# A two-layer hybrid trunk: the S5 input projection turned round and moved by DMA, two later slots in TensorE's order

## The chip, the cores and the metric

One core of one Trainium2 chip. The metric is the device time of one execution in microseconds (us). Engines: PE is TensorE, PEld its weight loads, DVE VectorE, ACT ScalarE, POOL GpSimd, SP SyncE, which here does nothing but issue DMAs.

## The reference

Two layers over one sequence of 512 tokens with 1024 features, all in float32. `h = modulate(rms_norm(x))` feeds every mixer through slices of one input matrix; the change touches the S5 mixer, the compressed keys of the sparse attention and a norm.

```python
x = x + 0.5 * g1 * swiglu(modulate(rms_norm(x, norm_ffn1), sh1, sc1), ffn1_w_in, ffn1_w_out)
h = modulate(rms_norm(x, norm_mix), sh2, sc2)
u_pool, u_q, u_kv, u_gate, u_s5 = split(h @ w_in)          # u_s5: 256 features
# S5: 16 groups of 16 features, 64 complex states each
bu = einsum('gph,bsgh->bsgp', b_bar, u_s5)                 # then a linear scan over the tokens
y  = einsum('ghp,bsgp->bsgh', c_mat, states).real + d_skip * u_s5
# compressed keys: blocks of 32 tokens every 16
k_cmp = rope(rms_norm(gelu((blk + pe) @ w1) @ w2, k_norm[0]))
x = x + g2 * (concat(norm(pool), norm(nsa), norm(y_s5)) @ w_out)
x = x + 0.5 * g3 * swiglu(modulate(rms_norm(x, norm_ffn2), sh3, sc3), ffn2_w_in, ffn2_w_out)
```

## The kernel before

Features of the residual and of `h` lie on the 128 partitions in 8 blocks, tokens along the free axis. A product of two float32 matrices is three matmuls (`mm3`): each operand is split into a rounded high part and a rest, and high x high, high x low and low x high are added up in PSUM. Weights come from DRAM through four slots (a loader issues the DMA on SP; a splitter makes the high part on ACT and the low part on DVE or POOL).

The order of the work is found when the program is built. `Sched` (class of `K`) holds a modelled clock for each engine; the stages are generators that yield the modelled time at which their last result is there, and the one with the earliest time issues next. So each engine gets one fixed list, executed in order. `act`, `tt`, `ptt`, `mm`, `tr` and `dma` issue an instruction (ACT, DVE, POOL, matmul, transpose on PE, DMA on SP) and return its modelled end. Adding a slack to a yielded time makes a stage resume later in the list: `calm` adds 450, `bcast_rstd` gets `NSLACK` (300) or `N2SLACK` (1300). Nothing waits for these times on the chip. A slack moves only the place in the lists.

In `mixer` the stages around the change come in this order. The projections of the values and keys (`proj_t`: tokens as the stationary operand, 256 columns moving) run, then the S5 projection. It is `proj_t` four times (lines 1973 to 1982), with the stationary operand `bass.DynSlice(s, 128, 4)`: every fourth token, starting at s. 96 matmuls of 128x256 go into four banks, four ACT evictions (`a5_evac`) put them into `a5` with tokens on the partitions, and `s5_chain` (line 1811) turns them into `U` by 8 transposes on PE in two banks and two ACT evictions. `U` holds features and token phase on the partitions: partition 32s + i, 8 blocks j, 128 chunks c of four tokens.

Then come the first product of the compressed keys (`compress(0)`, 16 matmuls of 128x64), the pool projection (48 matmuls of 128x512), the compressed values, another key projection, the queries and the attention. `s5_half` (one per half q of the S5 groups) multiplies `E` by `U` (two times four float32 matmuls of 128x128, which are two records each), rotates (DVE and POOL), scans (DVE, line 1770, 8 scans per half) and ends in the `Y` matmuls. `compress_post` (line 1586) takes the compressed keys through gelu, the second product with `w2` (one 64x64 matmul, after `calm`), the norm and the rotation, splits them into a high part `kh` (ACT) and a rest `kl` (DVE) and transposes both on PE. `norm_half` (line 832) sums squares, gets a row of statistics from PE, broadcasts it over the partitions with one matmul with ones (`bcast_rstd`), scales, and hands `h` to the first projections. Index 1 is the norm before the mixers.

```python
t = yield from proj_t(us5, b[:, 0:256], bass.DynSlice(s, 128, 4), 256, s == 3)
t = tr(b[:, j * 128:(j + 1) * 128], a5[:, jj].rearrange("p s c -> p (s c)"), ident)
```

Of the kernel before, what the change touches and what calls it, by code (L numbers as in the profile page):

```python
# [25 lines left out]
AF = mybir.ActivationFunctionType  # L26
# [292 lines left out]
NSLACK = 300.0  # L319
N2SLACK = 1300.0  # L320
LAT = {"pe": 150.0, "act": 100.0, "dve": 100.0, "pool": 120.0}
# [99 lines left out]
def kernel(ctx, tc, xT, c, ada, ws, sp, mp, bc, w1, c_cols, ada_pe, cst, out):  # L421
# [4 lines left out]
    K = Sched()  # L426
# [86 lines left out]
    def calm(t):  # L513

        return t + SLACK
# [23 lines left out]
    def wbank():  # L539
        n = yield from banks.get()  # L540
        return pbank(n)
# [265 lines left out]
    def bcast_rstd(rs, nb, dg, o, slack=0):  # L807

        for j in range(nb):
            t = ts(dg[:, j * 128:(j + 1) * 128], ident, rs[:, j:j + 1], None, OP.mult)  # L810
        yield t + slack
        return mm(o, ones, dg[:, :nb * 128])
# [12 lines left out]
    def norm_half(st, half):  # L825
# [20 lines left out]
        t = yield from bcast_rstd(ms, 2, sq, pb[:, :256], N2SLACK if "ops" in st and half != st["order"][0] else NSLACK)  # L846
# [658 lines left out]
    def mixer(l, st, nxt, s5):  # L1505
# [80 lines left out]
        def compress_post(kv, bn, b, t):  # L1586
            yield t
            (tn, ge), (t2n, kd) = yield from tmpn(F32, F32R)
            yield calm(act(ge[:, :64], b[:, :64], AF.Gelu_apprx_tanh))
# [140 lines left out]
        a5 = area[:, 4:6, :].rearrange("p a c -> p (a c)").rearrange("p (j s c) -> p j s c", j=8, s=4)  # L1730
# [3 lines left out]
        a5_ev, s5y_ev, e_done = [Ev() for _ in range(4)], Ev(), Ev()  # L1734
# [76 lines left out]
        def s5_chain():  # L1811
            for e in a5_ev:
                yield e
            yield s5["ev"]
            for q in range(2):
                yield calm(K.now)
                bn, b = yield from wbank()
                for j in range(4):
                    jj = 4 * q + j
                    t = tr(b[:, j * 128:(j + 1) * 128], a5[:, jj].rearrange("p s c -> p (s c)"), ident)  # L1820
                yield t
                t = act(U[:, 4 * q:4 * q + 4, :], b.rearrange("p (j c) -> p j c", j=4))
                banks.put(bn, t)
            yield calm(t)
# [148 lines left out]
        us5 = [take("s5"), take("s5")]  # L1973
        def a5_evac(bn, b, t, s):
            yield t
            t = act(a5[:, :, s, :], b[:, 0:256].rearrange("p (j c) -> p j c", j=8))
            banks.put(bn, t)
            K.set(a5_ev[s], t)
        for s in range(4):
            bn, b = yield from bank()  # L1980
            t = yield from proj_t(us5, b[:, 0:256], bass.DynSlice(s, 128, 4), 256, s == 3)
            K.spawn(a5_evac(bn, b, t, s))
# [640 lines left out]
```

## Time and profile before

| | |
|---|---|
| median of 3 runs | 2045.11 us (2043.85 to 2047.16) |
| the profiled execution | 2049.2 us, span 2047.2 us |
| mean granted TensorE clock | 0.983 |
| PE busy | 1963.0 us (96%), 12698 matmuls |
| PEld busy | 1769.3 us (86%) |
| DVE / ACT / POOL busy | 1600.8 (78%) / 895.9 (44%) / 636.9 (31%) us |
| chain that ended last | PE 76%, DVE 15%, POOL 5%, issue 2%, ACT 2%, DMA 1% |

Times in the views count from the start of the span. A group of a timeline is a run of like instructions: its start, its length, and in square brackets how long the engine stood idle just before it and what released it. `s` and `p` are tiles in SBUF and in PSUM. Line numbers are those of the kernel before: L502 is `mm`, L518 `tr`, L453 `act`, L462 `tt`, L489 `ptt`, L596 `dma`, L1770 the scan. In the changed kernel all helpers lie two lines lower, the scan three.

### The profile page before, as it was taken

To read this page: it belongs to the slowest core of one execution; us is meant where nothing else is said; L and a number is where in the kernel's file an instruction comes from. 1 tells how busy PE (TensorE), PEld (TensorE's weight loads), DVE (VectorE), ACT (ScalarE), POOL (GpSimd) and SP (SyncE) were. 2 spreads that over 40 slices of the span, in tenths; PEclk is the share of its full clock that TensorE was granted. 3 is DMA by queue.
4 is the path that set the end of the run, shared out by engine and by line. 5 is a ranking of instruction groups with operands and counts; after the bars stand their busy time and mean duration, and the time that the engine had idled before them with its cause. 6 is when DMAs were issued, how large, how long until landed. Compare 5 with 4: busy or idle time off the path is not lost.

```text
span 2047.2 us, 32760 instructions
## 1 busy us (share of the span) xinstructions
PE 1963.0 (96%) x12698; PEld 1769.3 (86%) x12698; DVE 1600.8 (78%) x2690; ACT 895.9 (44%) x1622; POOL 636.9 (31%) x849
## 2 busy tenths in 40 slices
PE   5999999999999899999999989999999998999999
PEld 3788888898988898999989888999978888898989
DVE  7679777776778788888889796778578779686866
ACT  3422222242566453534455343535327565453533
POOL 5039201954644520000022390056457362000000
PEclk9999999999998899999989999999999998999999
DMA  7658767531101125445322222313211011413232
GB/s 303 219 202 295 261 227 256 186 113 54 62 32 52 53 75 184 163 166 192 125 97 93 93 100 97 134 53 134 80 37 53 21 52 55 142 63 124 87 110 73
DMA packets 71147, 251.66 MB, mean 123 GB/s; under 512 B 8016, under 2 KB 10448, under 8 KB 70480
## 3 DMA queue, kind: packets, MB, share of 16 engines
q1 hardware_dynamic: 70992, 249.58, 34.8%
q8 instruction: 99, 1.62, 0.3%
q14 instruction: 56, 0.46, 0.1%
HBM read 247.45 MB, written 2.10 MB: 122 GB/s over the span
## 4 chain that ended last, share of the span: by engine, by line
PE 76%; DVE 15%; POOL 5%; issue 2%; ACT 2%; DMA 1%; SPq 0%; DVEq 0%; ACTq 0%; POOLq 0%
PE p L502 74%; DVE s L462 8%; DVE s L466 5%; POOL s L489 5%; PE p L518 3%; ACT s L453 2%; DVE s L1770 1%; DVE s L471 0%; DMA s<-in_ws_dram 0%; DMA s<-in_x_dram 0%; DVE p L2063 0%; DVE s L2063 0%; DVE s L481 0%; DVE s L473 0%; SPq L596 0%
## 5 line engine op out<-in xcount | busy, mean ns | idle before, releaser
L502 PE MATMUL p<-s,s 128*128 128x256 f32 (+5 forms) x12022 | 1911.4, 320 | 71.3 <-DVE s L462 28.2
L502 PEld LDWEIGHTS p<-s,s 128*128 128x128 f32 (+2 forms) x12022 | 1696.5, 194 | 253.6 <-DVE s L462 34.6
L453 ACT ACTIVATE s<-s 128x1024 fp32r<-128x1024 f32 (+4 forms) x900 | 615.1, 711 | 786.9 <-PE p L502 450.2
L462 DVE TENSOR_TENSOR s<-s,s 128x1024 fp32r<-128x1024 f32 (+7 forms) x804 | 754.1, 963 | 251.1 <-ACT s L453 240.8
L489 POOL TENSOR_TENSOR s<-s,s 128x256 f32<-128x256 f32 (+12 forms) x399 | 358.7, 920 | 291.7 <-DVE s L473 119.8
L489 POOL TENSOR_TENSOR s<-s 128x256 f32<-128x256 f32 (+4 forms) x244 | 178.7, 738 | 498.0 <-ACT s L453 330.0
L453 ACT ACTIVATE s<-p 128x512 f32<-128x512 f32 (+9 forms) x361 | 180.2, 520 | 269.3 <-PE p L502 196.5
L462 DVE TENSOR_TENSOR s<-p,s 128x512 f32<-128x512 f32 (+8 forms) x325 | 192.1, 604 | 62.1 <-ACT s L453 40.2
L466 DVE SCALAR_TENSOR_TENSOR s<-s,s 128x1024 f32<-128x1024 f32 (+3 forms) x179 | 204.0, 1146 | 1.7 <-DMA s<-in_ada_dram 0.5
L466 DVE SCALAR_TENSOR_TENSOR s<-p,s,s 128x512 f32<-128x512 f32 (+2 forms) x210 | 128.3, 619 | 52.7 <-PE p L502 48.5
L462 DVE TENSOR_TENSOR s<-s 128x256 f32<-128x256 f32 (+4 forms) x157 | 80.3, 522 | 16.5 <-POOL s L489 6.2
L498 POOL TENSOR_SCALAR s<-s 128x128 f32<-128x128 f32 (+9 forms) x58 | 34.3, 610 | 184.6 <-PE p L502 161.7
L518 PE MATMUL p<-s,s 128*128 128x128 f32 (+1 forms) x548 | 80.2, 275 | 9.7 <-DVE s L462 7.4
L518 PEld LDWEIGHTS p<-s,s 128*128 128x128 f32 (+1 forms) x548 | 64.6, 140 | 20.6 <-DVE s L462 8.0
L453 ACT ACTIVATE s<-p,s 128x512 f32<-128x512 f32 (+3 forms) x132 | 69.3, 533 | 25.3 <-DVE s L2063 15.8
L498 POOL TENSOR_SCALAR s<-s,s 128x512 f32<-128x512 f32 (+3 forms) x128 | 65.8, 535 | 22.4 <-DVE s L462 15.2
L466 DVE SCALAR_TENSOR_TENSOR s<-s,s,s 128x256 fp32r<-128x256 f32 (+3 forms) x124 | 66.9, 557 | 0.3 <-ACT s L453 0.2
L2063 DVE CUSTOM_DVE_ANT_0 p<-p,s 128x512 f32<-128x512 f32 (+3 forms) x128 | 60.5, 503 | 3.3 <-PE p L502 2.3
L453 ACT ACTIVATE s<-s,s 128x256 fp32r<-128x256 f32 x80 | 39.0, 504 | 27.3 <-DVE s L466 27.1
L466 DVE SCALAR_TENSOR_TENSOR s<-s,s,p 128x256 f32<-128x256 f32 (+1 forms) x88 | 42.3, 498 | 4.4 <-PE p L502 3.7
L462 DVE TENSOR_TENSOR s<-s,p 128x512 f32<-128x512 f32 (+1 forms) x35 | 20.5, 589 | 18.1 <-PE p L502 18.1
L466 DVE SCALAR_TENSOR_TENSOR s<-s 128x256 f32<-128x256 f32 (+3 forms) x72 | 32.4, 468 | 2.0 <-ACT s L453 1.6
(36 smaller groups left out, 212.0 us busy)
## 6 DMA issues: line engine op xcount, KB each, us to landing
s<-in_ws_dram SPq DMA_DIRECT2D x304, 512.0 KB, 4.2
s<-in_ada_dram SPq DMA_DIRECT2D x143, 512.0 KB, 4.9
s<-in_w_dram SPq DMA_DIRECT2D x4, 1024.0 KB, 6.2
s<-in_x_dram SPq DMA_DIRECT2D x8, 256.0 KB, 5.2
out_dram<-s SPq DMA_DIRECT2D x16, 128.0 KB, 1.7
s<-in_ws_dram SPq DMA_DIRECT2D x4, 420.0 KB, 3.0
s<-in_c_dram SPq DMA_DIRECT2D x2, 512.0 KB, 5.0
s<-in_bc_dram SPq DMA_DIRECT2D x2, 512.0 KB, 5.7
```

What stands on the lines that cost most here:

```text
L453: nc.scalar.activation(o, i, func, **kw)
L462: nc.vector.tensor_tensor(o, a, b, op)
L466: nc.vector.scalar_tensor_tensor(o, a, s, b, op0=op0, op1=op1, **kw)
L489: nc.gpsimd.tensor_tensor(o, a, b, op)
L498: nc.gpsimd.tensor_scalar(o, a, s1, s2, op0=op0, op1=op1)
L502: nc.tensor.matmul(o, l, r, start=start, stop=stop, **kw)
L518: nc.tensor.transpose(o, i, idn)
L1770: nc.vector.tensor_tensor_scan(zz, keep[:, 2, 4 * q + j:4 * q + j + 1].to_broadcast([128, 128]), zz, 0.0, op0=OP.mult, op1=OP.add)
L2063: nc.vector.tensor_tensor_reduce(b[:, :L], b[:, :L], mask, -0.125, 3.0e38, OP.add, OP.min, nmax[:, r:r + 1])
```

## The change

Three parts. (1) The S5 projection takes the weights as stationary operand and the 512 tokens as moving one, so features come out on the partitions: 48 matmuls of 128x512 into two banks. Two ACT evictions write `a5` with tokens sorted by phase, and 16 DMAs on SP, 32 partitions x 2 x 128 elements each (32 KB in rows of 512 bytes), copy `a5` to `U` within SBUF. The 8 transposes and their two evictions go, in each layer. (2) The `w2` product of the compressed keys and values gets a slack of 5000 in place of 450. (3) The broadcast of the first half of the norm before the mixers gets a slack of 2500 in place of 300.

```diff
+M1SLACK = 2500.0
+CMP_SLACK = 5000.0
...
-        t = yield from bcast_rstd(ms, 2, sq, pb[:, :256], N2SLACK if "ops" in st and half != st["order"][0] else NSLACK)
+        t = yield from bcast_rstd(ms, 2, sq, pb[:, :256], M1SLACK if idx == 1 and half == st["order"][0] else
+                                  N2SLACK if "ops" in st and half != st["order"][0] else NSLACK)
...
-            yield calm(act(ge[:, :64], b[:, :64], AF.Gelu_apprx_tanh))
+            yield act(ge[:, :64], b[:, :64], AF.Gelu_apprx_tanh) + CMP_SLACK
...
         def s5_chain():
-            for e in a5_ev:
-                yield e
+            yield u_ev
             yield s5["ev"]
-            for q in range(2):
-                yield calm(K.now)
-                bn, b = yield from wbank()
-                for j in range(4):
-                    jj = 4 * q + j
-                    t = tr(b[:, j * 128:(j + 1) * 128], a5[:, jj].rearrange("p s c -> p (s c)"), ident)
-                yield t
-                t = act(U[:, 4 * q:4 * q + 4, :], b.rearrange("p (j c) -> p j c", j=4))
-                banks.put(bn, t)
-            yield calm(t)
...
-        for s in range(4):
-            bn, b = yield from bank()
-            t = yield from proj_t(us5, b[:, 0:256], bass.DynSlice(s, 128, 4), 256, s == 3)
-            K.spawn(a5_evac(bn, b, t, s))
+        def s5_evac(bs, t):
+            yield t
+            for ft in range(2):
+                t = act(a5[:, ft], bs[ft][1].rearrange("p (c s) -> p s c", s=4))
+                banks.put(bs[ft][0], t)
+            yield t
+            Uv = U.rearrange("p (a j) c -> p a j c", a=2)
+            for s in range(4):
+                for j in range(4):
+                    t = dma(Uv[32 * s:32 * s + 32, :, j, :], a5[32 * j:32 * j + 32, :, s, :], 32 * 1024)
+            K.set(u_ev, t)
+        for k4 in range(2):
+            u = take("s5")
+            yield u["ev"]
+            for k in range(4 * k4, 4 * k4 + 4):
+                for i, b in enumerate(sbs):
+                    cc = slice((k % 4) * 256 + i * 128, (k % 4) * 256 + (i + 1) * 128)
+                    t = mm3(b[1], u["hi"][:, cc], u["lo"][:, cc], hh[:, k], hl[:, k], k == 0, k == 7)
+                    yield t - 170
+            done(u, t)
+        K.spawn(s5_evac(sbs, t))
         K.spawn(s5_chain())
         yield from compress(0)
```

TensorE of the first layer, kernel before, from the end of the first product of the compressed keys (`p_3607<-s_3093`) to the `w2` product (`p_3607<-s_3089,s_3681`). `p_3635` and `p_3658` are the banks of the transposes into `U`, `p_3685` to `p_3693` those of `E`, `p_3676` and `p_3677` those of the pool projection.

```order
L518 MATMUL p_3653<-s_64,s_3452 128x128 x4
L518 MATMUL p_3658<-s_64,s_3098 128x128 x4
...
L502 MATMUL p_3676<-s_3038,s_3445 128x512
L502 MATMUL p_3685<-s_3098,s_395 128x128 x4
L502 MATMUL p_3692<-s_3098,s_395 128x128 x4
...
L502 MATMUL p_3686<-s_3098,s_395 128x128 x4
L502 MATMUL p_3607<-s_3089,s_3681 64x64
L502 MATMUL p_3693<-s_3098,s_395 128x128 x4
```

The same place in the changed kernel (`p_3639`, `p_3646`, `p_3640`, `p_3647` are now the banks of `E`, `p_3621` and `p_3622` those of the pool projection, `s_3087,s_3632` the `w2` product).

```order
L520 MATMUL p_3627<-s_64,s_3450 128x128 x4
L504 MATMUL p_3622<-s_3071,s_3440 128x512
L504 MATMUL p_3622<-s_3072,s_3440 128x512
L504 MATMUL p_3622<-s_3071,s_3442 128x512
L504 MATMUL p_3639<-s_3096,s_395 128x128 x4
L504 MATMUL p_3646<-s_3096,s_395 128x128 x4
...
L504 MATMUL p_3640<-s_3096,s_395 128x128 x4
L504 MATMUL p_3647<-s_3096,s_395 128x128 x4
...
L504 MATMUL p_3558<-s_3087,s_3632 64x64
```

Between the end of the S5 projection and the first `E` matmul stand, in the first layer, 16 matmuls of the compressed keys, four groups of four other transposes and 6 matmuls of the pool projection (in the second 16, three groups and 9); the two groups of transposes into `U` are gone, and the `w2` product stands behind all of `E`. From the first `E` to the transposes of `kh` and `kl` there are 16 `E` matmuls, 42 of 128x512 and 8 of 128x64; before there were 16 and 36.

SyncE's list of the first layer, changed kernel: `s_3096` is the area that holds `a5` and `U`, `in_ws` and `in_w` are weights.

```order
L598 DMA s_3512<-in_ws_dram 128x1024
L598 DMA s_3533<-in_ws_dram 128x840
L598 DMA s_3096<-s_3096 32x2x128 x16
L598 DMA s_3603<-in_ws_dram 128x840
L598 DMA s_3091<-in_w_dram 128x2048
```

The 16 copies stand between two weight loads; each of the last 12 waits for its DMA lane, of which there are 8, and the first for the second eviction. On ACT a split of a weight tile (128x1024), which waits for the end of the S5 projection, stands ahead of the two evictions.

DVE of the first layer, kernel before: `s_3098` are the tiles of S5, `s_3682` is `kl` (the list names the scans SCALAR_TENSOR_TENSOR of L1770).

```order
L466 SCALAR_TENSOR_TENSOR s_3681<-p_3607,s_3715,s_65 64x64
L462 TENSOR_TENSOR s_3684<-p_3685,s_2411 128x512
L462 TENSOR_TENSOR s_3691<-p_3692,s_2411 128x512
L1770 SCALAR_TENSOR_TENSOR s_3098<-s_394,s_3098 128x128 x8
L462 TENSOR_TENSOR s_3682<-s_3681,s_3682 64x128
L1770 SCALAR_TENSOR_TENSOR s_3098<-s_394,s_3098 128x128 x4
```

The changed kernel (`s_3096` are the tiles of S5, `s_3633` is `kl`).

```order
L468 SCALAR_TENSOR_TENSOR s_3632<-p_3558,s_3680,s_65 64x64
L1773 SCALAR_TENSOR_TENSOR s_3096<-s_394,s_3096 128x128 x8
L464 TENSOR_TENSOR s_3699<-s_3486,s_3697 128x1024
L1773 SCALAR_TENSOR_TENSOR s_3096<-s_394,s_3096 128x128 x8
L464 TENSOR_TENSOR s_3638<-s_3096,s_2411 128x4x127
L464 TENSOR_TENSOR s_3633<-s_3632,s_3633 64x128
```

`kl` has moved behind eight more scans, a weight split and a multiply. The norm's broadcast moves 21 matmuls down in the first layer (12 matmuls of the feed-forward part still follow it, 33 before) and 3 down in the second, where it now ends the feed-forward part; there the statistics of the second half (two 128x1 matmuls) move from behind the first 12 matmuls of the projections to a place ahead of them, and on DVE the second half's sum and a weight split (128x1024) come to stand ahead of the first scaled tile.

## Rows read from the trace of the kernel before

**Rows 1.** Page: busy time of each engine, and the last chain's share by line.
```profile
PE 1963.0 (96%) x12698; PEld 1769.3 (86%) x12698; DVE 1600.8 (78%) x2690; ACT 895.9 (44%) x1622; POOL 636.9 (31%) x849
...
PE p L502 74%; DVE s L462 8%; DVE s L466 5%; POOL s L489 5%; PE p L518 3%; ACT s L453 2%; DVE s L1770 1%; DVE s L471 0%; DMA s<-in_ws_dram 0%; DMA s<-in_x_dram 0%; DVE p L2063 0%; DVE s L2063 0%; DVE s L481 0%; DVE s L473 0%; SPq L596 0%
```

**Rows 2.** Timeline of PE, first layer, from the S5 projection to the compressed keys.
```profile
447.23 22.66 PE L502 MATMUL p<-s,s 128*128 128x256 f32 x96
469.72 2.34 PE L502 MATMUL p<-s 128*128 128x64 f32 x20
471.89 0.61 PE L518 MATMUL p<-s,s 128*128 128x128 f32 x4
...
475.60 13.36 PE L502 MATMUL p<-s,s 128*128 128x512 f32 x73
...
492.85 0.27 PE L518 MATMUL p<-s,s 64*128 64x64 f32 x1 [3.69 <-DVE s L462]
```

**Rows 3.** Timeline of PE, second layer, the same places.
```profile
1447.65 22.65 PE L502 MATMUL p<-s,s 128*128 128x256 f32 x96
...
1493.29 0.37 PE L518 MATMUL p<-s,s 64*128 64x64 f32 x1 [3.68 <-DVE s L462]
```

**Rows 4.** PE's weight loads by form, 447.3 to 469.8 us: busy us, mean ns.
```profile
L502 PEld LDWEIGHTS p<-s,s 128*128 128x128 f32 x96 | 22.5, 329 | 0.0
```

**Rows 5.** Matmuls by form, 526 to 540 us (a projection by `proj_t`, contiguous tokens).
```profile
L502 PE MATMUL p<-s,s 128*128 128x256 f32 x99 | 13.0, 288 | 0.0
```

**Rows 6.** Timeline of ACT, feed-forward part: evictions of two successive groups of 48 matmuls.
```profile
186.01 0.60 ACT L453 ACTIVATE s<-p 128x512 f32<-128x512 f32 x1 [4.02 <-PE p L502]
...
197.21 0.60 ACT L453 ACTIVATE s<-p 128x512 f32<-128x512 f32 x1 [4.02 <-PE p L502]
```

**Rows 7.** ACT by form: weight splits, mean ns behind the comma.
```profile
L453 ACT ACTIVATE s<-s 128x1024 fp32r<-128x1024 f32 x390 | 411.8, 1058 | 552.5 <-PE p L502 450.2 <-issue 33.1 <-DMA s<-in_ws_dram 27.1
```

**Rows 8.** Timeline of SP at the start: issues back to back, and one alone.
```profile
0.72 3.70 SPq L596 DMA_DIRECT2D s<-in_x_dram  x8
...
6.54 0.33 SPq L596 DMA_DIRECT2D s<-in_c_dram  x1
```

**Rows 9.** DMA issues: KB each, median us from issue to landing.
```profile
out_dram<-s SPq DMA_DIRECT2D x16, 128.0 KB, 1.7
...
s<-in_cc_dram SPq DMA_DIRECT2D x1, 4.0 KB, 5.6
```

**Rows 10.** Stretch 493 to 497 us: busy PE, PEld, DVE, ACT, POOL, PEclk, DMA.
```profile
493.00:497.00 4.00, 4.00 (x13) 3.14 (x12) 4.00 (x11) 0.88 (x2) 4.00 (x1) 0.57 0.18 40
```

**Rows 11.** Timeline of DVE, first layer, scans and the rest of the compressed keys.
```profile
484.49 8.13 DVE L1770 TENSOR_TENSOR_SCAN s<-s,s 128x128 f32<-128x128 f32 x8
492.54 0.26 DVE L462 TENSOR_TENSOR s<-s,s 64x128 fp32r<-64x128 f32 x1
492.72 1.35 DVE L1770 TENSOR_TENSOR_SCAN s<-s,s 128x128 f32<-128x128 f32 x4
```

**Rows 12.** The first of these scans alone, and POOL's timeline beside it.
```profile
484.49 3.89 DVE L1770 TENSOR_TENSOR_SCAN s<-s,s 128x128 f32<-128x128 f32 x1
...
484.54 1.28 POOL L489 TENSOR_TENSOR s<-s,s 128x512 f32<-128x512 f32 x1
485.80 1.04 POOL L498 TENSOR_SCALAR s<-s 128x1024 fp32r<-128x1024 f32 x1
486.81 1.28 POOL L489 TENSOR_TENSOR s<-s,s 128x512 f32<-128x512 f32 x1
```

**Rows 13.** Timeline of PE where the mixers' first projections begin, both layers.
```profile
423.63 1.64 PE L502 MATMUL p<-s,s 128*128 128x256 f32 x12 [0.76 <-DVE s L466]
...
1419.91 0.38 PE L502 MATMUL p<-s,s 128*128 128x256 f32 x1 [1.35 <-ACT s L453]
```

**Rows 14.** Timeline of DVE there, second layer: a weight split, the second half's sum.
```profile
1419.49 1.22 DVE L462 TENSOR_TENSOR s<-s,s 128x1024 fp32r<-128x1024 f32 x1
...
1421.54 0.42 DVE L462 TENSOR_TENSOR s<-s 128x256 f32<-128x256 f32 x1
```

More of the change, by code (lines that the diff above doesn't have):

```diff
@@ L1727, in gate_chain @@
             K.set(g_ev[blkno], ts(gt, gt, 0.5, 0.5, OP.mult, OP.add))
-        a5 = area[:, 4:6, :].rearrange("p a c -> p (a c)").rearrange("p (j s c) -> p j s c", j=8, s=4)
+        a5 = area[:, 4:6, :].rearrange("p a (s c) -> p a s c", s=4)
         U = area[:, 6:8, :].rearrange("p a (j c) -> p (a j) c", c=128)
@@ L1733, in mixer @@
         Xi0 = area[:, 1, :].rearrange("p (j c) -> p j c", c=128)
-        a5_ev, s5y_ev, e_done = [Ev() for _ in range(4)], Ev(), Ev()
+        u_ev, s5y_ev, e_done = Ev(), Ev(), Ev()
         yn = s5["E"][:, 0].rearrange("p j c -> p (j c)").rearrange("p (t c) -> p t c", t=4)
@@ L1972, in mixer @@
                 K.spawn(blk_build(1, vcb, t))
-        us5 = [take("s5"), take("s5")]
-        def a5_evac(bn, b, t, s):
+        def s5_evac(bs, t):
             yield t
-            t = act(a5[:, :, s, :], b[:, 0:256].rearrange("p (j c) -> p j c", j=8))
-            banks.put(bn, t)
-            K.set(a5_ev[s], t)
-        for s in range(4):
-            bn, b = yield from bank()
-            t = yield from proj_t(us5, b[:, 0:256], bass.DynSlice(s, 128, 4), 256, s == 3)
-            K.spawn(a5_evac(bn, b, t, s))
+            for ft in range(2):
[7 more added lines that the diff above has]
+            K.set(u_ev, t)
+        sbs = []
+        for i in range(2):
+            b = yield from bank()
+            sbs.append(b)
+        hh, hl = st["h"]
+        for k4 in range(2):
[8 more added lines that the diff above has]
+        K.spawn(s5_evac(sbs, t))
         K.spawn(s5_chain())
```

## The prediction

> **What bounds the kernel now.** I read the page first, then the timelines of TensorE around the changed places, then the engines that it waits for there. PE is busy 1963.0 of 2047.2 us, and its matmuls hold 74% of the chain that ended last [rows 1]. So an edit pays what it takes off PE's own list or off PE's waits; work on other engines counts only where PE waits for it. In the stretch of the change the reader is to see three things: the S5 projection, 22.5 us long in either layer, without a gap [rows 2, 3]; after it a chain of small work with no wait; and a stall of 3.7 us at the transposes of the compressed keys, released by DVE [rows 2, 3].
>
> The sum is made against the profiled execution, 2049.2 us with a span of 2047.2, which lies 4.1 above the median of the runs. I take differences from it and put them on the median, 2045.1. A measurement can tell about 0.2%, 4.1 us, from no change: faster means under 2041.0, slower over 2049.2.
>
> **The projection.** The 96 matmuls of 128x256 start at 447.23 and the next group at 469.72: 22.5 us, 0.234 each [rows 2]. A projection of the same shape on contiguous tokens takes 0.13 (99 in 13.0) [rows 5]. What differs is the stationary operand, every fourth token: its loads take 329 ns, and 96 of them fill the 22.5 us [rows 4]. In the changed kernel it is a contiguous piece of the weights, and 48 matmuls of 128x512 do the work. Such a group of 48 has its eviction every 11.20 us in the feed-forward part [rows 6], 0.233 each. So 22.5 - 11.2 = **11.3 us less** per layer, all of it on PE, which has no wait there.
>
> The Trainium skill, "TensorE: Matmul & The Clock Gate", section "LDWEIGHTS (loading the stationary operand)", says that a load's time hangs on its number of columns alone, about 107 ns for 128 (its figure). By that rule the stride would not be the cause and the projection would keep its 22.5 us; the row of 329 ns speaks against it, and I take the row.
>
> **The transposes.** Eight of them go per layer: four take 0.45 (471.89 to the next group) [rows 2], so **0.9 less**. Their ACT evictions go too; nobody waited for them.
>
> **The new path to U.** Call the end of the S5 projection T. On ACT a weight split (1.06) [rows 7] stands ahead of two evictions of 0.60 [rows 6]: `a5` is complete at T + 2.3. SP then issues 16 copies. Eight issues back to back took 3.70, 0.46 each, one alone 0.33 [rows 8]; I take 0.46, so the last is issued at T + 2.3 + 15 x 0.46 = T + 9.2. No copy within SBUF stands in this trace. The nearest rows for its landing are 1.7 us for 128 KB out of SBUF and 5.6 for 4 KB into it [rows 9]; I take 2.0, close to the first, since neither source nor target is loaded. Then `U` is there at T + 11.2. PE meanwhile has 16 matmuls of 128x64 (0.22 each, two records of 0.11 [rows 2], 3.5), four groups of transposes (1.8) and 6 matmuls of 0.233 (1.4), 6.7 in all in the first layer; in the second three groups and 9 matmuls, 6.9. So the first `E` matmul waits **4.4 us** per layer. Queued behind it is all of PE, since the lists run in order. The bounds: with 0.33 and 1.7, T + 9.0 and a wait of 2.1; with 5.6 the eight lanes bind (below), a wait of about 10. Below nothing is excluded, as the copies can't start before T + 2.3 and there are 16 of them to issue.
>
> Behind the present stall of 3.69 us the granted clock is 0.57 over 4 us [rows 10], a mixture of 1.2 and 2.4 GHz, so 4 x 0.43 = 1.7 us are lost. A stall of like length should do the same: **1.7 more** (between 0 and 1.7).
>
> SP's other work: the weights behind the copies are queued some 9 us longer, but PE has 12 us and more of pool projection before it wants them. I cost it at nothing; a copy that lands 5.6 us late would use that cover up. On ACT, the split ahead of the evictions is the one already counted.
>
> **The compressed keys.** The first `E` matmul ran at 476.4 (three matmuls after 475.60). `kl` was ready 16.4 later (492.54 + 0.26) [rows 11], and PE came to it at 12.7, hence 3.69. In the changed order PE has 6 matmuls of 0.233 and 8 of 0.22 more on that way, 3.2: it comes at 16.0. On DVE `kl` now stands behind 16 scans, a split and a multiply. The first 8 scans start 8.1 after `E` and take 8.13, as POOL works beside them; four without much of that take 1.35 [rows 11], so the other 8 take 2.7; the split takes 1.2 [rows 14], the multiply, half as wide, about 1.0, `kl` 0.26: 8.1 + 8.1 + 2.7 + 1.2 + 1.0 + 0.3 = 21.4. The wait becomes 5.4, **1.7 more** per layer. Bounds: if no scan is held, the first 8 take 2.7 and the wait is gone (3.7 less); if the second 8 are held as the first are, it is 5.4 more. I take the middle, which the rows of the same code give. The slack itself costs nothing: the `w2` product only moves on PE, and its result still comes before the scans.
>
> **The norm.** First layer: the broadcast moves 21 matmuls down; 12 took 1.64 with a slow start [rows 13], so about 2.5 us later. PE waited 0.76 for the first scaled tile. If the tile hangs on the broadcast alone the wait grows by 2.5, if on DVE's other work by nothing; I take 1.2. There is no gain to have, as PE did not wait at the broadcast. Second layer: a split of 1.22 and a sum of 0.42 now stand ahead of the first scaled tile on DVE [rows 14], 1.64, of which three matmuls that now stand before the broadcast cover 0.36; the wait of 1.35 [rows 13] grows by 1.3 (0 to 2.2). Together **2.5 more**.
>
> **Sum.** Per layer -11.3 - 0.9 + 4.4 + 1.7 + 1.7 = -4.4; two layers -8.8; with the norm -6.3. The profiled execution would be 2042.9, the median 2045.1 - 6.3 = **2038.8 us**.
>
> **Rivals.**
>
> *A, the copies are hidden.* If SP issues faster than any row shows, or PE is slower on its way, the wait at `E` is nil and `kl` is as before: 2 x (-12.2) + 2.5 = -21.9, 2023. For it: the copies are small. Against it: 16 issues at 0.33 are 5.3 us by themselves, after 2.3 of ACT.
>
> *B, slower: the lanes bind.* There are 8 lanes, so the ninth copy waits for the landing of the first. With a landing of 5.6 [rows 9] the first lands at T + 7.9, the last is issued 7 x 0.46 later and lands at T + 16.7: a wait of 9.9 at `E`. Per layer -12.2 + 9.9 + 1.7 + 1.7 = +1.1, with the norm +4.7: 2050. It decides from a wait of 7.6 on, where two layers of (-12.2 + 7.6 + 3.4) and the norm's 2.5 cancel: a landing of 4.4 us. For it: the 4 KB transfer, the smallest shown, took 5.6. Against it: that one came from DRAM at the start; 1.7 is the only row with SBUF as source.
>
> *C, DVE is held for less.* The first scan took 3.89 us, as long as three POOL instructions beside it together, though one alone takes about 0.34 [rows 11, 12]. If in the new order it is held for one of them only (1.28), `kl` comes 2.3 earlier per layer (3.89 - 1.28 - 0.34), the wait is 3.1 instead of 5.4: 2038.8 - 4.6 = 2034. The Trainium skill, "SBUF — State Buffer", section "SBUF: two separate sides", has a lock on the port that DVE and GpSimd share, held for one whole instruction, which would let the scan in after one. The three instructions under one scan speak against it here [rows 12].
>
> *D, the projection is not shortened.* If the loads' 329 ns come from something other than the stride, 22.5 us stay per layer: 2038.8 + 22.6 = 2061. The 48-matmul groups of the same form at 11.2 [rows 6] speak against it.
>
> *E, the norm and keys cost nothing and the copies land at the lower bound.* Per layer -12.2 + 2.1 + 0.5, in all -19: 2026. It is the forecast with every unknown at its low end.
>
> **How the numbers follow.** Forecast 0.52 (own range 2031 to 2047: a wait at `E` of 2.1 to 6, a wait at `kl` 2 more or less), A 0.09, E 0.09, C 0.13, B 0.14, D 0.03. The range is to leave out 2 in 10: at the low end A and a little, at the high end D and half of B. 2023 to 2050 does so. Faster by over 0.2%: A, E and C whole and some six in ten of the forecast, 0.62. Within: the forecast's upper part and a third of B, 0.22. Slower: the rest, 0.16.
>
> **What would show it.** Right: a group of 48 matmuls of 128x512 of about 11.2 us in place of the 96; a wait at the first 128x128 matmuls of about 4 us, released by a DMA, and a clock near 0.6 behind it; at the 64x64 transposes a wait of about 5 released by DVE; the first projections of the second layer 1 us later after the feed-forward part. The forecast is wrong if the wait at `E` is under 2 or over 8, if issues on SP are much more than 0.46 apart (then the lanes bind), if the keys' wait is under 3, or if PE finds a new wait in the pool projection or the queries because weights came late behind the copies.

## The result, and the profile after

The changed kernel takes 2062.36 us (median of 4, 2057.83 to 2065.43) against 2045.48 for the kernel before (median of 4): a ratio of **1.0081 [1.0058, 1.0103]**, slower by 0.8%. The forecast of 2038.8 was wrong in sign and the time lies above the range. The profiled execution took 2060.6 us with a span of 2058.4, so 11.4 of the 17 us can be read from the profile.

Page of the changed kernel: busy time of each engine; and its DMA view: the copies, KB each, median us from issue to landing.

```profile
PE 1955.1 (95%) x12586; PEld 1753.6 (85%) x12586; DVE 1603.6 (78%) x2690; ACT 894.5 (43%) x1614; POOL 634.2 (31%) x849
...
s<-s SPq DMA_DIRECT2D x32, 32.0 KB, 1.9
```

PE is busy 7.9 us less than in [rows 1], with 112 matmuls fewer. TensorE's timeline (start, length, idle time just before and its releaser), first layer and then three places of the second; these rows answer to [rows 2, 3, 13].

```profile
422.51 2.10 PE L504 MATMUL p<-s,s 128*128 128x256 f32 x16 [0.29 <-DVE s L468]
...
445.58 11.44 PE L504 MATMUL p<-s,s 128*128 128x512 f32 x48
...
458.94 0.66 PE L520 MATMUL p<-s,s 128*128 128x128 f32 x4 [1.31 <-ACT s L455]
...
471.14 17.45 PE L504 MATMUL p<-s,s 128*128 128x128 f32 x76 [6.03 <-DMA s<-s]
491.21 0.27 PE L520 MATMUL p<-s,s 64*128 64x64 f32 x1 [0.89 <-ACT s L455]
496.58 0.36 PE L520 MATMUL p<-s,s 64*128 64x64 f32 x1 [5.09 <-DVE s L464]
...
1419.49 1.52 PE L504 MATMUL p<-s,s 128*128 128x1 f32 x5 [2.59 <-DVE s L464]
1421.80 4.42 PE L504 MATMUL p<-s,s 128*128 128x256 f32 x19 [0.80 <-DVE s L468]
...
1472.45 5.55 PE L504 MATMUL p<-s,s 128*128 128x128 f32 x19 [5.33 <-DMA s<-s]
...
1500.53 0.36 PE L520 MATMUL p<-s,s 64*128 64x64 f32 x1 [8.85 <-DVE s L464]
```

The projection is 11.44 long instead of 22.66, and the two groups of transposes into `U` are gone. Two waits stand in their place: at the first `E` matmul 6.03 and 5.33, where there was none, and at the transposes of `kh` and `kl` 5.98 (0.89 + 5.09) and 8.85, where there were 3.69 and 3.68. What PE waited for there, in the timelines of SP and ACT (first layer) and of DVE and POOL (both layers):

```profile
460.83 10.80 SPq L598 DMA_DIRECT2D s<-s  x16
...
458.17 1.67 ACT L455 ACTIVATE s<-s 128x256 fp32r<-128x256 f32 x3 [5.88 <-POOL s L491]
459.75 1.06 ACT L455 ACTIVATE s<-p 128x512 f32<-128x512 f32 x2
...
482.64 2.62 DVE L1773 TENSOR_TENSOR_SCAN s<-s,s 128x128 f32<-128x128 f32 x8
486.14 2.31 DVE L464 TENSOR_TENSOR s<-s,s 128x1024 fp32r<-128x1024 f32 x1 [0.88 <-POOL s L500]
488.37 6.53 DVE L1773 TENSOR_TENSOR_SCAN s<-s,s 128x128 f32<-128x128 f32 x8
...
1484.12 7.23 DVE L1773 TENSOR_TENSOR_SCAN s<-s,s 128x128 f32<-128x128 f32 x8
1493.18 6.51 DVE L1773 TENSOR_TENSOR_SCAN s<-s,s 128x128 f32<-128x128 f32 x8
...
482.86 3.25 POOL L500 TENSOR_SCALAR s<-s 128x1024 fp32r<-128x1024 f32 x1 [0.86 <-PE p L504]
...
1483.48 1.05 POOL L500 TENSOR_SCALAR s<-s 128x1024 fp32r<-128x1024 f32 x1
1484.50 3.45 POOL L491 TENSOR_TENSOR s<-s,s 128x512 f32<-128x512 f32 x5
```

The 16 copies take 10.80 us to issue, 0.67 each. The granted clock, from the windows of the changed kernel (start and end, length, busy PE, PEclk, DMA share, GB/s): behind the first layer's wait at `E` (8 us, then one microsecond of them), behind its wait at the keys, behind the second layer's wait at `E`, and over the second layer's attention. Attention in the kernel before is the fence after it.

```profile
472.00:480.00 8.00, 8.00 (x38) 0.64 0.53 191
476.00:477.00 1.00, 1.00 (x5) 0.50 0.77 320
500.00:508.00 8.00, 8.00 (x51) 0.69 0.17 61
1472.00:1480.00 8.00, 7.55 (x40) 0.64 0.54 195
1559.00:1642.00 83.00, 80.25 (x444) 0.94 0.10 32
```

```profile
1559.00:1634.00 75.00, 72.98 (x432) 1.00 0.12 36
```

The 0.64 is a mean of two levels. By single microseconds the clock is at 0.50, its lower level (1.2 GHz), from the first `E` matmul at 471.1 to about 477.7 us, and at full speed from there on; in the second layer it is low until about 1477.8. Behind the stall of [rows 10] it was low for 3.4 us, from about 493.2 to 496.6.

**Where the time went.** I added up 4 us windows from the mixers' start to their end (in the kernel before 400.0 to 705.3 and 1400.1 to 1702.5): idle is length less PE's busy time, "clock" is busy x (1 - granted clock), "work" is the rest, PE's work at full clock. First layer / second layer, in us:

| kernel | length | idle | clock | work |
|---|---|---|---|---|
| before | 305.3 / 302.4 | 19.5 / 18.3 | 9.3 / 5.7 | 276.5 / 278.4 |
| before, another execution (e7) | 305.3 / 305.4 | 19.1 / 17.8 | 9.9 / 10.0 | 276.3 / 277.6 |
| after | 306.6 / 315.0 | 27.7 / 29.8 | 14.2 / 19.8 | 264.8 / 265.4 |
| e2, norm's slack undone | 306.6 / 307.4 | 28.1 / 25.8 | 14.2 / 16.5 | 264.3 / 265.0 |
| e15, that slack undone in layer 2 only | 305.4 / 306.1 | 27.5 / 26.0 | 13.5 / 15.2 | 264.4 / 265.0 |
| e1, `w2` slack undone | 316.8 / 318.6 | 32.9 / 31.0 | 16.5 / 18.9 | 267.5 / 268.6 |
| e3, both slacks undone | 316.9 / 316.1 | 33.4 / 31.2 | 16.6 / 17.1 | 266.9 / 267.8 |
| e9, e2 with two issuing queues | 301.1 / 302.7 | 24.1 / 22.9 | 13.0 / 14.3 | 264.0 / 265.5 |
| e16, e9 with a short `w2` slack | 313.6 / 311.5 | 29.5 / 26.9 | 16.7 / 16.4 | 267.3 / 268.2 |

Work fell by 24.7 over both layers; 19.7 came back as waits and 19.0 as a lower clock, and the rest of the program, outside these stretches, is 2.7 shorter: the 11.2 by which the span grew. Of the waits 11.4 stand at `E` and 7.5 more at the keys. Of the clock, 6.1 lie behind `E` (2.7 in 8 us at 0.64 in the second layer, 3.4 from 464 to 480 us in the first), 3.1 more than before behind the keys, and 4.8 (80.25 x 0.06) in the second layer's attention; about 5 are scattered, near the 4.3 by which two executions of the kernel before differ in the second layer. Part of the 4.8 may be chance too: e7, the other execution, has 0.98 over its attention there, 1.5 us lost, where the one compared with lost none.

### The profile page after: what moved, and what is told of

It is laid out like the page before. It is cut to its first block, busy times and chain, and to the rows that moved or that the text cites. A ratio compares the mean times of both kernels' runs of the same rounds, so it can differ in the third digit from the quotient of the medians.

```text
span 2058.4 us, 32592 instructions
## 1 busy us (share of the span) xinstructions
PE 1955.1 (95%) x12586; PEld 1753.6 (85%) x12586; DVE 1603.6 (78%) x2690; ACT 894.5 (43%) x1614; POOL 634.2 (31%) x849
## 5 line engine op out<-in xcount | busy, mean ns | idle before, releaser
L504 PE MATMUL p<-s,s 128*128 128x256 f32 (+4 forms) x11926 | 1904.2, 321 | 82.9 <-DVE s L464 30.4
L504 PEld LDWEIGHTS p<-s,s 128*128 128x128 f32 x11926 | 1677.0, 192 | 270.5 <-DVE s L464 35.7
L464 DVE TENSOR_TENSOR s<-s,s 128x1024 fp32r<-128x1024 f32 (+8 forms) x804 | 755.6, 966 | 225.8 <-ACT s L455 217.9
L491 POOL TENSOR_TENSOR s<-s,s 128x256 f32<-128x256 f32 (+12 forms) x399 | 352.5, 903 | 288.0 <-ACT s L455 81.1
L455 ACT ACTIVATE s<-p 128x512 f32<-128x512 f32 (+6 forms) x353 | 177.6, 524 | 264.1 <-PE p L504 180.9
L464 DVE TENSOR_TENSOR s<-p,s 128x512 f32<-128x512 f32 (+7 forms) x325 | 191.8, 604 | 69.1 <-ACT s L455 42.5
L520 PE MATMUL p<-s,s 128*128 128x128 f32 (+2 forms) x532 | 80.8, 279 | 17.0 <-DVE s L464 13.9
L520 PEld LDWEIGHTS p<-s,s 128*128 128x128 f32 (+2 forms) x532 | 64.9, 142 | 30.2 <-DVE s L464 14.4
L2073 DVE CUSTOM_DVE_ANT_0 p<-p,s 128x256 f32<-128x256 f32 (+3 forms) x128 | 60.9, 503 | 9.5 <-PE p L504 9.2
```

The source lines that it names most:

```text
L455: nc.scalar.activation(o, i, func, **kw)
L464: nc.vector.tensor_tensor(o, a, b, op)
L491: nc.gpsimd.tensor_tensor(o, a, b, op)
L504: nc.tensor.matmul(o, l, r, start=start, stop=stop, **kw)
L520: nc.tensor.transpose(o, i, idn)
L2073: nc.vector.tensor_tensor_reduce(b[:, :L], b[:, :L], mask, -0.125, 3.0e38, OP.add, OP.min, nmax[:, r:r + 1])
```

## The experiments

All are made from the changed kernel unless the heading says "before". Ratios are to the kernel before, run beside them. Letters of theories in the quoted expectations are their own, not those of the prediction's rivals; what follows is said in words.

### Which of the three parts costs the time

**e1_calm**: the `w2` slack undone.
```diff
-            yield act(ge[:, :64], b[:, :64], AF.Gelu_apprx_tanh) + CMP_SLACK
+            yield calm(act(ge[:, :64], b[:, :64], AF.Gelu_apprx_tanh))
```


> The changed kernel with the w2 product's slack back at 450; kl stands ahead of the S5 scans on VectorE again. Theory K (the later place of the compressed keys costs what the traces show at their transposes: waits of 0.9 + 5.1 and 8.9 us, and a halved clock behind each for about 4 us): the wait falls to under 2 us per layer, the clock behind it stays up, and 12 us of waits and some 5 of clock come back: about 2046 us. Theory C (the copies alone make the loss, 6.0 and 5.3 us at the first E matmul with a halved clock behind; the keys' wait only moves to the next late result): within 3 us of the changed kernel's 2062.

Measured 2074.06, 1.0131 [1.0115, 1.0148]. The wait at the keys was gone, and the kernel was 10 us slower than after, not faster: no theory had that.

**e2_norm**: the norm's slack undone.
```diff
-M1SLACK = 2500.0
+M1SLACK = 300.0
```


> The changed kernel with the norm's broadcast back at a slack of 300. Both theories: no difference over 2 us (2060 to 2064); the traces show the waits at the mixers' first projections at 0.76 + 0.40 before and 0.29 + 0.28 after in the first layer, 1.35 + 0.87 before and 2.59 + 0.80 after in the second. If the order of the second layer that this slack brings is what loses its clock in the attention, 2054.

Measured 2052.92, 1.0027 [1.0014, 1.0040]: the norm's slack costs 11 us (0.0054 of 2045), though at its own place PE's waits hardly differ. The table puts it into the second layer (307.4 for 315.0). There the wait at the keys is smaller, and the first scans are shorter; PE, DVE and POOL of e2, second layer:

```profile
1493.41 0.27 PE L520 MATMUL p<-s,s 64*128 64x64 f32 x1 [0.88 <-ACT s L455]
1498.76 0.37 PE L520 MATMUL p<-s,s 64*128 64x64 f32 x1 [5.08 <-DVE s L464]
...
1484.84 2.61 DVE L1773 TENSOR_TENSOR_SCAN s<-s,s 128x128 f32<-128x128 f32 x8
...
1485.07 3.24 POOL L500 TENSOR_SCALAR s<-s 128x1024 fp32r<-128x1024 f32 x1 [0.85 <-PE p L504]
```

The second layer now runs as the first does: eight scans in 2.61 instead of 7.23, and 5.96 at the keys instead of 8.85. The slack, 80 us further up in the list (1419 against 1500 us), had changed which of DVE and POOL came first at the scans: here the scans start at 1484.84 and POOL's split at 1485.07, while in the changed kernel the split was at work (1483.48 to 1484.53) when the first scan came at 1484.12.

**e15_norm_l0**: the norm's slack in the first layer only.
```diff
-        ... M1SLACK if idx == 1 and half == st["order"][0] else
+        ... M1SLACK if idx == 1 and l == 0 and half == st["order"][0] else
```


> The changed kernel with the norm's slack of 2500 in the first layer alone. If the second layer's new order (kl's wait 8.9 instead of 5.1, norm 1.2 more) is what the slack costs: 2051 to 2055, as with the slack undone in both. If the first layer's move costs half of it, 2057 to 2059; if it is chance of the clock, over 2060.

Measured 2053.38, 1.0023 [1.0013, 1.0034], as e2. So the whole cost of that slack is what it does to the second layer's order.

**e3_proj**: both slacks undone, the projection and the copies alone (the edits of e1 and e2).

> Both slacks back, only the projection and the copies changed. Theory K: about 2046 us as with the keys' slack alone back. Theory C: within 3 us of 2062. In either, the wait at the first E matmul stays at 5 to 6 us in both layers, released by a DMA.

Measured 2075.66, 1.0133 [1.0109, 1.0157]. TensorE, first layer:

```profile
485.83 0.34 PE L520 MATMUL p<-s,s 64*128 64x64 f32 x2
...
502.42 0.49 PE L504 MATMUL p<-s,s 128*128 128x128 f32 x2 [3.72 <-DVE s L464]
506.81 8.58 PE L504 MATMUL p<-s,s 128*128 128x128 f32 x55 [3.90 <-DVE s L464]
```

The keys' wait is gone and stands at the two `Y` groups instead, 3.72 + 3.90. That explains 1.6 us a layer against e2, not the 21.7 by which e3 is slower than it (0.0106 of 2045); the rest comes later, in attention (below, at e16).

**e4_slacks** and **e8_cmp**: before, with both slacks and with the `w2` slack alone, old projection. The edit of e8; e4 has `M1SLACK = 2500.0`.
```diff
+M1SLACK = 300.0
+CMP_SLACK = 5000.0
...
-            yield calm(act(ge[:, :64], b[:, :64], AF.Gelu_apprx_tanh))
+            yield act(ge[:, :64], b[:, :64], AF.Gelu_apprx_tanh) + CMP_SLACK
```


> The kernel before with the two slacks of the change alone, the projection and the transposes as they were. Theory K: kl stands behind all 16 scans, the wait at the transposes grows from 3.7 to 6 to 9 us per layer with a longer halved clock behind it: 2052 to 2060. Theory C: no loss, 2043 to 2047.

> The kernel before with the later w2 product alone (kl behind all 16 scans), the norm's slack as before. With both slacks it was 9 us slower. Theory L: the wait at kl is 5 to 9 instead of 3.7 us per layer and the Y matmuls, now right behind it, no longer wait 1.3: 0 to 6 us slower. If the norm's slack made all of the 9 us, no difference over 2 us.

Measured 2055.65, 1.0050 [1.0034, 1.0066], and 2055.57, 1.0024 [1.0010, 1.0039]. On the old projection the `w2` slack costs 5 us; on the new one it gains 22 (e3 to e2). Its worth hangs on the rest of the program. The kernel before, once more beside e8 (**e7_before**), took 2050.94 and gave the second row of the table: its clock losses differ from those of the first row by 0.6 and 4.3, little enough to leave most of the second layer's loss standing.

> The kernel before, once more, for a second trace: how far the halved clock of the attention differs between executions of one kernel. Work out of 4 us stretches in the first trace: 9.3 us lost to the clock in the first mixer and 5.7 in the second. Theory L: within 4 us of these. Theory H: the same. If they differ by 8 us or more, the loss of 14 us of clock in the second mixer of the changed kernel is chance.

### The copies

**e9_queues**: e2 with the copies issued in turn by SP and ACT.
```diff
-    def dma(o, i, nbytes):
-        nc.sync.dma_start(o, i)
+    def dma(o, i, nbytes, q=None):
+        (q or nc.sync).dma_start(o, i)
...
-                    t = dma(Uv[...], a5[...], 32 * 1024)
+                    t = dma(Uv[...], a5[...], 32 * 1024, nc.scalar if j % 2 else nc.sync)
```


> The changed kernel with the norm's slack undone (2053, 6 to 7 over the kernel before), and the 16 copies issued by two engines, 8 by SyncE and 8 by ScalarE; TensorE's list is the same. Theory D (the S5 chain decides the stage: eviction, copies, E, then some 25 us of rotation and scans on VectorE, which delivers kl, Y and the next key norms in order): the issues of 0.65 us run side by side, U is there 4 to 5 us earlier, the wait at the first E falls from 6 to 1 or 2 us, and all that hangs on VectorE's block comes as much earlier: 10 us of waits and 3 of clock over two layers, 2038 to 2043. Theory W (the wait only moves to the next place): within 3 us of 2053.

Measured 2043.41, 0.9984 [0.9966, 1.0001], 8.8 us less than e2 by the ratios. TensorE, SP, ACT and DVE of e9, first layer, and the window behind the wait at `E`:

```profile
469.84 14.07 PE L504 MATMUL p<-s,s 128*128 128x128 f32 x76 [2.48 <-DMA s<-s]
...
486.50 0.27 PE L520 MATMUL p<-s,s 64*128 64x64 f32 x1 [0.86 <-ACT s L455]
491.86 0.36 PE L520 MATMUL p<-s,s 64*128 64x64 f32 x1 [5.09 <-DVE s L464]
...
463.09 5.69 SPq L598 DMA_DIRECT2D s<-s  x8
...
464.31 4.70 ACTq L598 DMA_DIRECT2D s<-s  x7
...
477.94 2.62 DVE L1773 TENSOR_TENSOR_SCAN s<-s,s 128x128 f32<-128x128 f32 x8
...
468.00:476.00 8.00, 6.16 (x44) 1.00 0.63 210
```

Each queue still takes 0.67 to 0.71 for an issue, side by side, so the pitch is the issuing queue's; a limit on lanes or on the transfers would not have halved. The wait at `E` falls to 2.48, the one at the keys stays at 5.95.

**e13_after_queues**: the same on the changed kernel.

> The changed kernel, whole, with its copies issued by two engines (SyncE and ScalarE), its norm slack as changed. Theory D: as without the norm's slack, 4 to 5 us of S5 chain per layer come back, 2050 to 2055. If the second layer's loss has nothing to do with when U is there, 2057 to 2060.

Measured 2057.66, 1.0037 [1.0024, 1.0050], 9 us less than after by the ratios and 3.9 by the two profiled spans (2054.5 and 2058.4). From e9 to e13 the norm's slack costs 11 us again. The wait at `E` fell to 2.48 in the first layer, but not in the second. TensorE of e13 there, and its DMA issues from 1464 to 1466.4 us (KB each, median us to landing):

```profile
1464.38 0.46 PE L504 MATMUL p<-s,s 128*128 128x128 f32 x2 [1.93 <-DMA s<-s]
1470.83 4.60 PE L504 MATMUL p<-s,s 128*128 128x128 f32 x17 [5.99 <-DMA s<-s]
...
s<-in_w_dram SPq DMA_DIRECT2D x1, 1024.0 KB, 5.8
s<-s ACTq DMA_DIRECT2D x4, 32.0 KB, 4.7
```

`E` waited 7.92 there instead of 5.33: ACT began its copies 2.8 us after SP, SP went on to the next weight load meanwhile, and the last copies landed 4.7 us after their issue and not 1.9. That the load held them back is the likely reading; no run separates it. So the first mixer is 4.5 us shorter than in after and the second 1.2 longer: the second queue pays where its copies don't meet a load.

**e14_early_evac**: e9, with the evictions planned earlier and the copies without a yield ahead of them.
```diff
-            yield t
+            yield t - 1500.0
...
-            yield t
             Uv = U.rearrange("p (a j) c -> p a j c", a=2)
...
-            K.set(u_ev, t)
+            K.set(u_ev, t + 2800.0)
```


> The changed kernel without the norm's slack, two issuing engines, and the two evictions of the S5 projection placed on ScalarE ahead of the splits of other tiles that delay them by 1.9 us, the copies right behind them. Theory D: U is there 2 us earlier than with two engines alone, the wait of 2.5 at the first E goes to under 1: 2034 to 2041, under the kernel before. Against it: the list is planned anew, and its order in the stage is now that of the second layer of the changed kernel, with a wait of 8.9 at kl; if that order is what costs, 2045 to 2052.

Measured 2064.36, 1.0074 [1.0054, 1.0094]. No wait on a copy was left at `E`; PE waited for ACT at the transposes ahead of it instead (3.32 and 4.62), and 8.25 and 8.24 at the keys. The waits moved and grew; attention is longer too (at e16).

### DVE's block, and the order behind it

**e10_tr**, **e11_queues_tr** and **e12_before_tr**: the transposes of `kh` and `kl` later, in e2, in e9 and in before.
```diff
-            yield calm(tt(kl, xn[:, None, :].to_broadcast([64, 2, 64]), f(kh), OP.subtract))
+            yield tt(kl, xn[:, None, :].to_broadcast([64, 2, 64]), f(kh), OP.subtract) + 4000.0
```


> The changed kernel with the norm's slack undone, and the transposes of kh and kl placed behind 15 matmuls of the next key projection (a slack of 4000 behind kl). Theory D: VectorE's block ends no earlier, so the waits of 0.9 + 5.1 us at the transposes turn into waits of 3 to 6 us at the Y matmuls: within 4 us of 2053. If the wait at the transposes was worth its length, 2037 to 2043.

> Both: two issuing engines and the later transposes. Theory D: as the two queues alone or a little better, 2036 to 2042, with waits of under 3 us at E, at the transposes and at Y. If the two edits are independent and each worth its wait: 2026 to 2032.

> The kernel before with the later transposes alone (9 more matmuls of the pool projection and 6 of 128x64 ahead of them). Theory D: the wait of 3.7 us at kl falls to 1 or less and the one of 1.3 at Y grows to 3 or 4; within 3 us of the kernel before. If each wait is worth its length and its clock, 8 to 10 us faster.

Measured 2066.69, 1.0102 [1.0080, 1.0125]; 2058.00, 1.0047 [1.0032, 1.0062]; 2053.71, 1.0031 [1.0013, 1.0050]. TensorE of e10, first layer:

```profile
500.67 0.27 PE L520 MATMUL p<-s,s 64*128 64x64 f32 x1 [2.44 <-DVE s L464]
...
507.53 9.16 PE L504 MATMUL p<-s,s 128*128 128x128 f32 x57 [2.27 <-DVE s L464]
```

The later transposes wait less than half as long, and most of what PE saved there it waits at `Y`: 4.7 in all instead of 6.0. In e11 the two waits are 2.45 and 2.34. All three are slower than without the edit. In e10 and e11 the waits can't be the reason, as their sum fell; attention is longer there (at e16). Only e12 leaves attention as it was, at 74.9 us. TensorE of e12, first layer, then the wait at `Y` in before:

```profile
492.98 0.27 PE L518 MATMUL p<-s,s 64*128 64x64 f32 x1 [1.17 <-DVE s L462]
497.84 0.79 PE L502 MATMUL p<-s,s 128*128 128x128 f32 x2 [2.16 <-DVE s L462]
500.70 4.63 PE L502 MATMUL p<-s,s 128*128 128x128 f32 x20 [2.06 <-DVE s L462]
...
506.42 4.52 PE L502 MATMUL p<-s,s 128*128 128x128 f32 x30 [1.27 <-DVE s L462]
```

There the wait did move: 1.17 at the keys and 4.22 at `Y`, for 3.69 and 1.27.

**e5_late_y** and **e6_late_ey**: e3 with `Y` later (the first edit), and with `E` later as well (both).
```diff
-            yield calm(t)
+            yield t + 12000.0
...
-            K.set(u_ev, t)
+            K.set(u_ev, t + 8000.0)
```


> The projection and the copies of the change, both of its slacks undone, and a slack of 12000 ahead of the Y matmuls of each half of S5, so that they stand about 30 matmuls of 128x256 further down; the first E matmul stays where it is. Theory L (TensorE's list no longer holds enough work beside the S5 chain of eviction, copies, E, rotation and scans, so that the time taken out of the projection comes back as waits at what that chain delivers, with a halved clock behind each): the waits of 3.7 + 3.9 and 3.7 + 3.6 us at the Y matmuls go, the one of 5 to 6 at E stays, some 15 us and 5 of clock come back: 2052 to 2060, against 2076 without this slack. Theory H (the halved clock of the attention makes the loss, whatever the waits): over 2068.

> As the run before this one, and a slack of 8000 on the event that says U is there, so that the first E matmul stands behind 36 instead of 6 matmuls of the pool projection. Theory L: no wait over 1 us at E, kl and Y in the stage, the projection's and transposes' 24 us stay saved: 2026 to 2036, faster than the kernel before. Theory H: 2050 or more.

Measured 2063.82, 1.0063 [1.0044, 1.0081], and 2068.90, 1.0091 [1.0076, 1.0107]. TensorE of e5:

```profile
508.74 17.64 PE L504 MATMUL p<-s,s 128*128 128x512 f32 x130 [7.25 <-DVE s L468]
```

The `Y` waits are gone and their sum stands at one place further on, where a key norm on DVE releases PE; e6 removes the wait at `E` too and has 7.75 there, then 2.14 and 3.45 behind DVE further on. PE can be kept busy ahead of the block, but DVE's list has to be run through before it goes on.

**e16_queues_w2**: e9 with `CMP_SLACK = 1500.0`.

> The changed kernel without the norm's slack, two issuing engines, and the w2 product's slack at 1500 instead of 5000: kl stands behind 8 of the 16 scans and the transposes behind 33 matmuls of the pool projection, as in the kernel before. Theory D (the time from the first E to the Y matmuls is set by VectorE's block, some 29 us, and the matmuls in between fill some 22): the waits between E and Y keep their sum of about 6 us per layer, of which 2 to 3 at kl and 3 to 5 at Y; the time is within 5 us of the run with two engines and the later product, 0.2% under the kernel before to 0.1% over it. If the later product was the gain itself, 1% or more over the kernel before, as without two engines.

Measured 2062.54, 1.0069 [1.0052, 1.0087]. TensorE and the window of the first layer's attention of e16, then that window of e9:

```profile
496.87 0.79 PE L504 MATMUL p<-s,s 128*128 128x128 f32 x2 [3.56 <-DVE s L464]
500.52 9.86 PE L504 MATMUL p<-s,s 128*128 128x128 f32 x55 [2.86 <-DVE s L464]
...
562.00:653.00 91.00, 83.98 (x463) 0.94 0.06 18
```

```profile
560.00:640.00 80.00, 77.02 (x451) 0.98 0.10 32
```

The waits between `E` and `Y` sum to 6.42 against 5.95 in e9, so where the `w2` product stands hardly matters to them. But the window of attention is 91 us and not 80: 4.0 more idle (7.02 against 2.98), 3.5 more lost to the clock (83.98 x 0.06 against 77.02 x 0.02) and 3.5 more busy time at full clock, of which 12 more matmuls in the window (463 against 451) explain a part. Over the whole first mixer, where the matmuls are the same, the table has e16 at 5.4, 3.7 and 3.3 more than e9.

From its last 128x280 matmul to the first 128x128 of the next group attention takes 75.6 us in e2, e9, e15 and the first layer of after, 83.6 in the second layer of after, and 87 to 89 in e1, e3 and e16. The planner lists the work in another order there, and more of it between these marks: 449 matmuls in e16 and 448 in the second layer of after for 427 in e9. The 14 of 128x512 and 8 transposes that e16 has more are some 4 us by their usual pitch (0.233 and 0.11), so about 9 of its 13 us are slower running. Why that order runs slower inside stays open; no run changed the attention's order alone.

By the same marks this order sets the runs on the new projection apart. Attention is long in both layers, 80 to 89 us, in e1, e3, e5, e6, e10, e11, e14 and e16 (ratios 1.0047 to 1.0133); in the second alone, 83.6 and 82.2, in after and e13; in neither in e2, e9 and e15 (0.9984 to 1.0027). The eight hold the largest misses of the expectations: e6 was to take 2026 to 2036 us, e11 and e14 at most 2042 by their first theory, and e10 and e16 as much as e2 and e9 to within 4 and 5. This compares runs that differ in their waits too and is no test of the order; but what an edit at the keys or at `Y` does by itself can't be read from these eight times.

## Why the prediction was wrong, point by point

**The projection and the transposes: right.** -12.2 per layer was forecast, and work fell by 11.7 and 13.0. The loads, by form over 445.6 to 457 us of the changed kernel (busy us, mean ns):

```profile
L504 PEld LDWEIGHTS p<-s,s 128*128 128x128 f32 x48 | 9.0, 188 | 2.1
```

In the kernel before, the contiguous projection of [rows 5] has the same (526 to 540 us):

```profile
L502 PEld LDWEIGHTS p<-s,s 128*128 128x128 f32 x110 | 13.3, 188 | 1.0 <-issue 1.0
```

A contiguous load takes 188 ns, one with the stride 329 [rows 4], both of 128 columns; in the kernel before both serve matmuls of 128x256. Rival D falls. (The loads overlap, as 96 of 329 ns would be 31.6 us; what the stride costs is the pitch, 0.234 for 0.131 us.) The rule of the Trainium skill, "TensorE: Matmul & The Clock Gate", section "LDWEIGHTS (loading the stationary operand)", that the time goes by columns alone, does not hold here.

**The new path to `U`: mechanism right, size wrong.** The step "0.46 each" failed: an issue took 0.67, and in the first layer `a5` was complete at T + 4.0 (T = 456.8; evictions end at 460.81), not T + 2.3, since splits that waited on POOL stood ahead; in the second layer T + 2.0. One thing was better: the first `E` matmul needs 13 of the copies, not 16 (its four groups then follow the last four copies). T + 4.0 + 12 x 0.67 + 1.9 = T + 13.9; it ran at T + 14.3. PE came at T + 8.3, hence 6.0 for the 4.4 forecast, 5.3 in the second layer: +2.6 over both. Rival B ended on the right side for the wrong reason: the landing was 1.9, so the lanes never bound.

**The clock behind `E`: "a stall of like length should do the same", 1.7.** It did 3.4 and 2.7, because PE ran at the low clock for 6.5 and 5.3 us and not for 3.4. The wait was longer than the stall of [rows 10], and the last copies set the pace of the first four groups of `E`; which of the two kept the clock low no run separates. +2.7.

**The keys: sign right, undersized.** The step "21.4" failed: `kl` was there 25.4 after the first `E` (496.58 against 471.14). `E` ran at the low clock, so the scans started 11.5 behind it instead of 8.1; in e9, with the clock at 1.00 behind `E`, they start at 8.1 (477.94 against 469.84), as forecast. The terms behind that start were wrong in both directions: the first eight scans took 2.62 and not 8.1, the second eight 6.53 and not 2.7, the split with its wait for POOL 3.1 and not 1.2. In e9 they add up to 22.0 all the same, and its wait of 5.95 for the 5.4 is luck. In the first layer of after PE, at the low clock too, took 19.2 on its way rather than 16.0, so the wait was 5.98. In the second layer it was 8.85, as the first eight scans took 7.23 and the second 6.51. Waits +4.1 over the forecast, and +3.1 of clock behind them that had no term.

Rival C had DVE held by one POOL instruction. The rows show both sides held in turn. In the first layer eight scans ran in 2.62 and POOL's split beside them took 3.25, which takes 1.05 in the second; there POOL's split was at work when the first scan came, and the scans took 7.23 while POOL ran its next five operations. The Trainium skill, "SBUF — State Buffer", section "SBUF: two separate sides", has a lock by which the one that starts first holds the other off; the rows agree as to who waits, but the split was held over several scans, not one instruction.

**The norm: "together 2.5 more" at its entry.** It was 0.6 there (0.29 + 0.28 for 0.76 + 0.40, and 2.59 + 0.80 for 1.35 + 0.87). But the term counted only the entry. **This is the step that cost most:** the sum took "two layers" as twice the first and let it end at the keys, as if every list behind kept its order. e2 and e15 show that the norm's slack costs 11 us in the second layer, by its scans, its wait at the keys and its attention. Without it (e2) the forecast's -8.8 would still have stood against +5.5 (1.0027): the rest of the miss is in the terms above and in lower clock that had no term. Over both mixers e2 loses 15.7 more to the clock than before (30.7 against 15.0), where 3.4 were forecast.

**Not forecast at all:** two `Y` waits of 1.27 went (-2.5), a wait on ACT of 1.31 came.

By these terms the 17.7 between -6.3 and the profile's +11.4 is 5.3 at `E` with its clock, 7.2 at the keys with theirs, 4.8 of clock in the second layer's attention, and 5.0 of scattered clock that no run separates from what two executions of one kernel differ by. All others together are -4.7 (norm -1.9, `Y` and ACT -1.2, work -0.3, other idle time +1.4, outside the mixers -2.7).

The best version found, e9, has the projection's 25 us of work less and is still not separable from the kernel before.

## What to carry to other kernels

When a step leaves the critical path, time its replacement from the first issue to the first reader, on one queue, in order: here the wait behind 16 issues of 0.67 took back 11.4 of the 24.7 us that the projection gave, and a second queue returned 9 us in e9, but not in the layer where its copies met a weight load (e13). Where an engine's in-order block releases another, moving the waiting instruction moves the wait (e12); a shorter block was not tried. Where a planner sets the lists, a slack is an edit to everything behind it: compare the order of all later stages, in each layer by itself, before pricing it at its own place.

## What the runs showed of the hardware that was not expected

- A copy within SBUF of 32 partitions x 2 rows of 512 bytes took 0.67 us to issue on SP, twice the 0.33 of a load by itself and half as much again as the 0.46 of loads back to back [rows 8]. SP and ACT issued side by side at 0.67 to 0.71 each.
- Whether POOL or DVE is the one held up where scans and POOL operations meet changed the same eight scans from 2.62 to 7.23 us.
- Behind a wait of 6.0 us PE ran at the low clock (0.50) for some 6.5 us, behind one of 5.3 for 5.3, behind the 3.7 of [rows 10] for 3.4. Behind the 2.48 of e9's first layer the clock stayed at 1.00; behind the 2.21 of its second layer it was 0.50 for some 3 us.
- Four such copies that ACT issued around a weight load of 1024 KB on SP (e13) landed 4.7 us after their issue; in e9 and in the changed kernel it was 1.9.
